# A decoder block's first stage rebuilt: x in two halves, modulation by pairs of chunks, eight accumulators, products of ones in pauses

## The chip, the cores and the metric

The kernel runs on one core of a Trainium2 chip. The metric is the device time of one execution in microseconds (us); the kernel before took 1197.91 us, the median of three runs from 1197.79 to 1198.57. The engines have one instruction queue each and run them in order: TensorE (PE in the profile; its weight loads are listed apart as PEld), VectorE (DVE), ScalarE (ACT), GpSimd (POOL) and SyncE (SP), which here issues every DMA. They wait for each other on semaphores.

## What is computed

One layer of a decoder block over 1024 tokens of width 1024. Only its opening is touched by the change:

```python
cond = jax.nn.silu(c)
mod = cond @ w_ada + b_ada                      # 6 x 1024
sh_a, sc_a, gt_a, sh_m, sc_m, gt_m = jnp.split(mod, 6)
h = rms_norm(x, g_attn_pre) * (1 + sc_a) + sh_a
proj = h @ w_in                                 # 1024 x 2304
```

Behind that stand two attention mixers over `proj`, an output projection, a residual and a squared-ReLU MLP of width 4096. All operands are float32. A product of large matrices is made of three TensorE passes, since each operand is split into a high part and the rest: high by high, high by low, low by high.

## The kernel before

The tokens lie in 8 blocks (`tb`) of 128, the model width in 8 chunks (`k`) of 128. The six units `u` of `w_in` are 384 columns wide (`UW`). A unit's projection of a block accumulates in one PSUM bank over the 8 chunks, with three products of 128x128 by 128x384 for each chunk (L771, L772 and L774 in `proj_mm`; "a triple" below). A block's accumulator is then read out by `evac` (rotary embedding, splits into high and low parts, and transposes of queries and keys on TensorE, L724 and L736), and attention starts from these with its score products (L997).

The first stage does four things. It loads x, squares it for the norm (`x_block`, L553), scales it by the norm (L558), transposes it on TensorE (eight products per block, L568) and copies it to `xnT` (L573). It loads the 2048 columns of `w_ada` that make `sh_a` and `sc_a`, and multiplies them with `cond`: partly on TensorE, as products whose moving operand has a single column (L615), partly on VectorE into `acc_a` (L626, L628), whose 128 rows are then added up by products with a column of ones (L635). Out of that come scale and shift of one chunk (L640, L641). It modulates x with them (L645) and splits the result into `hw`, high part on ScalarE (L651), low part on GpSimd (L654). And it multiplies unit 0.

Before the change, five blocks (`FIRST`) take part while `w_ada` arrives: chunk by chunk, `mod_chunk` makes the coefficients, and the five accumulators of `first_unit` take that chunk in. The remaining three blocks are transposed later, wait in PSUM for all eight chunks' coefficients (L580, L583, L593, L596) and are multiplied as ordinary tiles (`proj_tile`).

The order of instructions on each engine is not written out: `Sched` is a planner that runs when the program is built. Each step has a listed duration, dependences, buffers that it takes and gives back, and a priority; at each point the planner takes the step that can start first by its own clocks. The order that comes out is then fixed in the program. The listed durations decide only the order; on the chip each instruction waits on semaphores. TensorE's steps stand in named streams, of which `prefer` takes one first. Loads go through SyncE, in the order of the priorities from `pri()`; a load whose buffer is still in use holds up those behind it. Buffers are `stg` (3 tiles), `wa`, and `w_st` for `w_in`.

Of the kernel before, what the change touches and what calls it, by code (L numbers as in the profile page):

```python
# [134 lines left out]
class Sched:  # L135


    def __init__(self):
        self.clk = dict(PE=0.0, ACT=0.0, DVE=0.0, POOL=0.0, SP=0.0)
        self.queue = {e: [] for e in ("ACT", "DVE", "POOL", "SP")}  # L140
        self.pe = {}
        self.launch = []
        self.seq = 0
        self.dma = 0.0

# [84 lines left out]
    def run(self, prefer):  # L230
        while True:
# [72 lines left out]
def hybrid_block(ctx: ExitStack, tc: tile.TileContext, x, positions, w_ada, b_ada, g_attn_post, w_in, w_out,  # L304
# [110 lines left out]
    FIRST = 5  # L415
# [4 lines left out]
    xnT = p0.tile([P, KC, FIRST * P], F32, name="xnT")  # L420
    r_wa, r_xs, r_acc = Res(4), Res(2), Res(3)
# [6 lines left out]
    e_c = load(lambda: nc.sync.dma_start(head[:], consts[:, 0:HEAD]), 106496, prio=pri())  # L428
    wa_t, wa_e, sent = {}, {}, {}

    def load_ada(k):
        def emit():
            wa_t[k] = p0.tile([P, KC, 2, P], F32, name="wa", tag="wa", bufs=4)
            for i in range(2):
                nc.sync.dma_start(wa_t[k][:, :, i], ada_view[:, :, i * D + k * P:i * D + (k + 1) * P])

        def issued():
            sent[k].t = 0.0
        sent[k] = Ev()
        wa_e[k] = load(emit, 1048576, takes=[(r_wa, 1)], prio=pri(), after=issued)  # L440
# [3 lines left out]
    def load_x(tb, deps=()):  # L444
        r = r_stg if tb % 2 == 0 else r_xs

        def emit():
            x_t[tb] = stage("x_sb") if tb % 2 == 0 else p0.tile([P, D], F32, name="x_sb", tag="x_sb", bufs=2)
            nc.sync.dma_start(x_t[tb][:], x[tb * P:(tb + 1) * P])
        x_e[tb] = load(emit, 524288, deps, takes=[(r, 1)], prio=pri())  # L450
# [3 lines left out]
    def load_w(u, k, prio=None, deps=()):  # L454
# [13 lines left out]
        w_rawe[u, k] = load(emit, 196608, deps, takes=[(r_wst, 1)], prio=pri() if prio is None else prio)  # L468

    def split_w(u, k):  # L470
# [10 lines left out]
        if u == 0:  # L481
            w_e[u, k] = op("POOL", t_ptt(UW), lo(G), [e], gives=[(r_wst, 1)], prio=3)
# [3 lines left out]
    for tb in range(2):  # L486
        load_x(tb)
    e_posi = load(lambda: nc.sync.dma_start(posi[:], positions), 4096, prio=pri())
    load_ada(0)
    for tb in range(2, FIRST):  # L490
        load_x(tb)
    load_w(0, 0)
    for k in range(1, KC):
        load_ada(k)
        load_w(0, k)
    for tb in range(FIRST, TB):
        load_x(tb, [sent[KC - 2 if tb == FIRST else KC - 1]])

    e_init = op("DVE", 0.3, lambda: (V.memset(ones[:], 1.0), V.memset(nhalf[:], -0.5)), prio=0)
# [40 lines left out]
    def f_sin():  # L540
# [3 lines left out]
    e = op("ACT", 3.0, f_sin, [e], prio=8)  # L544
    e_rope = op("DVE", 0.15, lambda: V.tensor_scalar(sinw[:, :, 0], sinw[:, :, 1], -1.0, None, ALU.mult), [e],
                prio=8)

    e_xn = []

    def x_block(tb):  # L550
# [8 lines left out]
        box, eh, d_all, evs_ = {}, [], [], []  # L559

        def hv():
            return x_t[tb][:].rearrange("p (k t) -> p k t", k=KC)
        r_x_ = r_stg if tb % 2 == 0 else r_xs
        for g in range(2):
# [4 lines left out]
            d = pe_op("xt", 0.7, tr, [e], takes=[(r_t, 1)], gives=[(r_x_, 1)] if g and tb < FIRST else [])  # L569
            d_all.append(d)  # L570
            if tb < FIRST:
                def ev(fn, g=g):
                    return lambda: fn(xnT[:, 4 * g:4 * g + 4, tb * P:(tb + 1) * P], box[g][:])  # L573
                e_xn.append(op("ACT", t_ps(512), ev(A.copy), [d], gives=[(r_t, 1)], prio=2))
            else:
                def ev(eng, g=g):
                    def f():
                        for k in range(4 * g, 4 * g + 4):
                            if eng is A:
                                A.activation(hv()[:, k], box[g][:, k - 4 * g], AF.Identity,  # L580
                                             bias=s_a[:, k:k + 1], scale=g_a[:, k:k + 1])
                            else:
                                V.tensor_scalar(hv()[:, k], box[g][:, k - 4 * g], g_a[:, k:k + 1],  # L583
                                                s_a[:, k:k + 1], ALU.mult, ALU.add)
                    return f
                evs_.append((d, ev))
        for d, ev in evs_:

            eh.append(op(("ACT", "DVE"), (1.4, 1.3), (ev(A), ev(V)), d_all + [e_gs[k] for k in range(KC)],
                         gives=[(r_t, 1)], prio=1))  # L590
        if tb >= FIRST:
            def hi(fn):
                return lambda: fn(hw[:, tb, 0], x_t[tb][:])  # L593

            def lo(eng):
                return lambda: eng.tensor_tensor(hw[:, tb, 1], x_t[tb][:], hw[:, tb, 0].bitcast(F32), ALU.subtract)  # L596
            e = op(("ACT", "DVE"), (t_sb(D), t_d2(D)), (hi(A.copy), hi(V.tensor_copy)), eh, prio=1)
            e2 = op(("DVE", "POOL"), (t_dv(D), t_ptt(D)), (lo(V), lo(G)), [e], gives=[(r_x_, 1)], prio=1)
            e_h[tb] = [e, e2]

    e_gs, e_h, e_hh, e_hl = {}, {}, {}, {}
    NF0 = FIRST * P
    ADA_PE = (8, 2, 2, 2, 2, 2, 2, 2)

    def mod_chunk(k):
        b = {}
        e = None
        jp = ADA_PE[k]
        ej = None

        def pm0():
            b["ps"] = px.tile([P, 2], F32, name="pm", tag="x")
            for i in range(2):
                for j in range(jp):
                    T.matmul(b["ps"][:, i:i + 1], wa_t[k][:, j, i], cond[:, j:j + 1], start=(j == 0), stop=(j == jp - 1))  # L615
        if jp:
            e = pe_op("mod", 0.426 * jp, pm0, [wa_e[k], e_cond], takes=[(r_x, 1)],
                      gives=[(r_wa, 1)] if jp == KC else [])
            if jp < KC:
                ej = op("DVE", 0.07, lambda: V.tensor_tensor(bb[:, k], bb[:, k], b["ps"][:], ALU.add), [e, e_cols],  # L620
                        gives=[(r_x, 1)], prio=1)
        for j in range(jp, KC):
            def f(j=j):
                if j == jp:
                    b["acc"] = p0.tile([P, 2, P], F32, name="acc_a", tag="acc_a", bufs=3)
                    V.tensor_scalar(b["acc"][:], wa_t[k][:, j], cond[:, j:j + 1], None, ALU.mult)  # L626
                else:
                    V.scalar_tensor_tensor(b["acc"][:], wa_t[k][:, j], cond[:, j:j + 1], b["acc"][:], ALU.mult, ALU.add)  # L628
            e = op("DVE", 0.4 if j > jp else 0.26, f, [wa_e[k], e_cond] if j == jp else [e] + ([ej] if ej and j == KC - 1 else []),
                   takes=[(r_acc, 1)] if j == jp else [], gives=[(r_wa, 1)] if j == KC - 1 else [], prio=3)  # L630

        def pm():
            b["ps"] = px.tile([P, 2], F32, name="pm", tag="x")
            for i in range(2):
                T.matmul(b["ps"][:, i:i + 1], b["acc"][:, i], ones[:, 0:1], start=True, stop=True)  # L635
        if jp < KC:
            e = pe_op("misc", 0.43, pm, [e, e_init], takes=[(r_x, 1)], gives=[(r_acc, 1)])

        def gs():
            V.tensor_scalar(g_a[:, k:k + 1], b["ps"][:, 1:2], bb[:, k, 1:2], cols[:, 8 + k:9 + k], ALU.add, ALU.mult)  # L640
            V.tensor_scalar(s_a[:, k:k + 1], b["ps"][:, 0:1], bb[:, k, 0:1], None, ALU.add)  # L641
        e = e_gs[k] = op("DVE", 0.26, gs, [e, e_cols] + ([ej] if ej else []), gives=[(r_x, 1)], prio=0)
        h = xnT[:, k]
        e = op("ACT", t_sb(NF0) + 2 * AP_COST,
               lambda: A.activation(h, h, AF.Identity, bias=s_a[:, k:k + 1], scale=g_a[:, k:k + 1]),  # L645
               [e] + e_xn, prio=0)

        hb, ks = h.rearrange("p (b t) -> p b t", t=P), slice(k * P, (k + 1) * P)

        def hi(fn):  # L650
            return lambda: fn(hw[:, 0:FIRST, 0, ks], hb)  # L651

        def lo(eng):
            return lambda: eng.tensor_tensor(hw[:, 0:FIRST, 1, ks], hb, hw[:, 0:FIRST, 0, ks].bitcast(F32),  # L654
# [5 lines left out]
    for tb in range(FIRST):  # L660
        x_block(tb)
# [1288 lines left out]
```

## Time and profile before

| what | value |
|---|---|
| median of three runs | 1197.91 us |
| the profiled execution | 1197.14 us, of which its span from first to last instruction 1195.4 us |
| granted TensorE clock, mean over the span | 0.988 |
| the first product of unit 0 (acc, L771) | starts at 28.70 us |
| the first score product of attention (s_ps, L997) | starts at 86.8 us |
| the MLP's products (mlp_ps) | from 565.1 us on |

The page gives busy time by engine, a strip of 40 slices of the span, the chain of work that ended last, and groups of instructions. Times in a timeline are from the start of the span: start, duration, engine, line, operation, tile written and tiles read, count, and in brackets how long the engine had stood idle and what ended that. A float32 product with a single moving column (L615, L635) is recorded twice, so 32 records are 16 instructions. A matmul's recorded duration contains its way through the array; what a product costs in a row of them is the distance from one start to the next.

### The profile page before, as it was taken

To read this page: it belongs to the slowest core of one execution; us is meant where nothing else is said; L and a number is where in the kernel's file an instruction comes from. 1 tells how busy PE (TensorE), PEld (TensorE's weight loads), DVE (VectorE), ACT (ScalarE), POOL (GpSimd) and SP (SyncE) were. 2 spreads that over 40 slices of the span, in tenths; PEclk is the share of its full clock that TensorE was granted. 3 is DMA by queue.
4 is the path that set the end of the run, shared out by engine and by line. 5 is a ranking of instruction groups with operands and counts; after the bars stand their busy time and mean duration, and the time that the engine had idled before them with its cause. 6 is when DMAs were issued, how large, how long until landed. Compare 5 with 4: busy or idle time off the path is not lost.

```text
span 1195.4 us, 17424 instructions
## 1 busy us (share of the span) xinstructions
PE 1143.5 (96%) x6064; PEld 998.0 (83%) x6064; DVE 881.3 (74%) x1794; ACT 666.6 (56%) x1411; POOL 264.6 (22%) x325
## 2 busy tenths in 40 slices
PE   7879999999998998999899999999999999999996
PEld 6869999989998896888688888888888888888885
DVE  4977667666789897667888955479763797646998
ACT  6457666556666787667657533473325643246542
POOL 6534655465655333111100000000000000000002
PEclk9889999999999999999999999999999999999999
DMA  9621333213231422555296126952268511586103
GB/s 290 189 60 60 89 98 97 77 52 102 76 87 54 125 53 77 179 201 204 113 381 246 36 73 238 340 168 62 81 218 284 191 36 53 179 287 220 36 19 141
DMA packets 104423, 166.53 MB, mean 139 GB/s; under 512 B 11152, under 2 KB 56336, under 8 KB 104336
## 3 DMA queue, kind: packets, MB, share of 16 engines
q1 hardware_dynamic: 104336, 165.42, 41.8%
q8 instruction: 48, 0.79, 0.3%
q14 instruction: 39, 0.32, 0.1%
HBM read 137.08 MB, written 28.31 MB: 138 GB/s over the span
## 4 chain that ended last, share of the span: by engine, by line
PE 76%; DVE 13%; issue 4%; ACT 3%; POOL 3%; DMA 1%; SPq 0%; DVEq 0%; POOLq 0%; ACTq 0%
PE mlp_ps L1773 16%; PE mlp_ps L1774 16%; PE mlp_ps L1772 16%; PE pj L771 4%; PE pj L774 3%; PE pj L772 3%; PE s_ps L997 3%; PE o_ps L1131 1%; PE pt_ps L1100 1%; DVE acc_a L628 1%; PE y_ps L1348 1%; PE y_ps L1350 1%; PE pm L615 1%; PE y_ps L1349 1%; PE pt_ps L1103 1%
## 5 line engine op out<-in xcount | busy, mean ns | idle before, releaser
L1772 PE MATMUL mlp_ps<-hw 128*128 128x512 f32 x896 | 350.4, 391 | 0.4 <-ACT hw L1534 0.4
L1773 PE MATMUL mlp_ps<-hw 128*128 128x512 f32 x896 | 349.2, 390 | 1.1 <-DVE hw L1540 1.1
L1774 PE MATMUL mlp_ps<-hw 128*128 128x512 f32 x896 | 349.1, 390 | 0.0
L1773 PEld LDWEIGHTS mlp_ps<-hw 128*128 128x128 f32 x896 | 168.6, 188 | 36.9 <-DVE hw L1540 1.4
L1772 PEld LDWEIGHTS mlp_ps<-hw 128*128 128x128 f32 x896 | 168.6, 188 | 36.1 <-ACT hw L1534 0.8
L1774 PEld LDWEIGHTS mlp_ps<-hw 128*128 128x128 f32 x896 | 168.5, 188 | 35.1
L1543 DVE TENSOR_TENSOR hw<-w,hw 128x1024 fp32r<-128x1024 f32 x96 | 114.6, 1219 | 93.5 <-ACT hw L1536 93.3
L1536 ACT CAST hw<-w 128x1024 fp32r<-128x1024 f32 x96 | 97.4, 1046 | 129.9 <-PE mlp_ps L1774 93.2
L1872 POOL TENSOR_TENSOR st<-st,nhalf 128x1 f32<-128x1 f32 x8 | 7.8, 978 | 602.8 <-DVE st L1870 602.8
L771 PE MATMUL pj<-w_hl,hw 128*128 128x384 f32 x344 | 128.2, 373 | 10.0 <-DVE sk L717 10.0
L774 PE MATMUL pj<-w_hl,hw 128*128 128x384 f32 x344 | 117.4, 341 | 0.0
L772 PE MATMUL pj<-w_hl,hw 128*128 128x384 f32 x344 | 117.1, 341 | 0.0
L1536 ACT CAST hw<-u 128x1024 fp32r<-128x1024 f32 x48 | 48.6, 1051 | 64.6 <-PE mlp_ps L1774 64.6
L1118 DVE TENSOR_TENSOR ph<-pt_ps,ph 128x512 fp32r<-128x512 f32 (+1 forms) x110 | 68.8, 643 | 18.5 <-ACT ph L1114 17.6
L771 PEld LDWEIGHTS pj<-w_hl,hw 128*128 128x128 f32 x344 | 65.8, 191 | 11.8 <-issue 8.7
L1543 DVE TENSOR_TENSOR hw<-u,hw 128x1024 fp32r<-128x1024 f32 x48 | 57.0, 1217 | 18.2 <-ACT hw L1536 18.2
L1114 ACT CAST ph<-pt_ps 128x512 fp32r<-128x512 f32 (+1 forms) x110 | 59.2, 560 | 13.8 <-PE pt_ps L1103 9.8
L772 PEld LDWEIGHTS pj<-w_hl,hw 128*128 128x128 f32 x344 | 66.2, 192 | 0.8 <-issue 0.2
L774 PEld LDWEIGHTS pj<-w_hl,hw 128*128 128x128 f32 x344 | 65.7, 191 | 0.0
L1027 POOL TENSOR_SCALAR p_sb<-p_sb,den 128x128 f32<-128x128 f32 (+3 forms) x64 | 50.1, 786 | 70.2 <-DVE den L1025 46.8
L1830 DVE TENSOR_TENSOR yacc<-yacc,mlp_ps 128x512 f32<-128x512 f32 x96 | 62.1, 680 | 3.3 <-PE mlp_ps L1774 3.3
L1022 ACT ACTIVATE p_sb<-p_sb,mn 128x128 f32<-128x128 f32 (+3 forms) x64 | 49.9, 780 | 20.4 <-DVE mn L1015 16.6
(209 smaller groups left out, 2202.6 us busy)
## 6 DMA issues: line engine op xcount, KB each, us to landing
hw<-s_dram SPq DMA_DIRECT2D x84, 512.0 KB, 4.5
wa_st<-in_w_ada SPq DMA_DIRECT2D x32, 512.0 KB, 4.0
w<-in_w_up SPq DMA_DIRECT2D x32, 512.0 KB, 5.4
w<-in_w_down SPq DMA_DIRECT2D x32, 512.0 KB, 8.0
s_dram<-hw SPq DMA_DIRECT2D x28, 512.0 KB, 4.3
x_sb<-in_x SPq DMA_DIRECT2D x16, 512.0 KB, 6.2
wa<-in_w_ada SPq DMA_DIRECT2D x16, 512.0 KB, 7.0
w_st<-in_w_in SPq DMA_DIRECT2D x32, 192.0 KB, 4.7
```

Source lines behind the costliest of these rows:

```text
L771: T.matmul(ps, hw[:, tb, 0, t], w[:, 0], start=(k == 0), stop=False)
L772: T.matmul(ps, hw[:, tb, 0, t], w[:, 1], start=False, stop=False)
L774: T.matmul(ps, hw[:, tb, 1, t], w[:, 0], start=False, stop=(k == KC - 1))
L1027: lambda b=b, qi=qi: G.tensor_scalar(rec.p[qi], rec.p[qi], b["den"][:], 1.0, ALU.mult, ALU.mult), [e], prio=1))
L1114: A.copy(b["ph"][:, 0, :w], b["pt"][:, :w])
L1118: V.tensor_tensor(b["ph"][:, 1, :w], b["pt"][:, :w], b["ph"][:, 0, :w].bitcast(F32), ALU.subtract)
L1536: A.copy(out[j][0], flat(src[j]))
L1543: V.tensor_tensor(out[j][1], flat(src[j]), out[j][0].bitcast(F32), ALU.subtract)
L1772: T.matmul(ps[m][:], sh, mh, start=starts and k == 0, stop=False, **kw)
L1773: T.matmul(ps[m][:], sh, ml_, start=False, stop=False, **kw)
L1774: T.matmul(ps[m][:], sl, mh, start=False, stop=k == 3, **kw)
L1830: e = op("DVE", t_dv(512), lambda: V.tensor_tensor(y(), y(), ps[m][:], ALU.add), [e, ml.e_y[tb, n]], gives=gives, prio=1)
```

## The change

x is loaded, normed and transposed for all eight blocks: blocks 0 to 3 ahead of the first `w_ada` tiles, 4 to 7 behind the first four of them. `w_ada` arrives in 16 tiles, four for each pair of chunks, each with a quarter of the rows for that pair's 512 columns (two DMAs, in runs of 256 columns instead of 128), and the modulation is made by pairs of chunks (`mod_group`). For the first pair all of it is done by single-column products on TensorE (32), for the other three pairs half (16) and the rest on VectorE, added up by four products with ones. The transposes' copies and the modulated x are divided between ScalarE and VectorE; GpSimd has neither the low parts of `hw` nor those of unit 0's weights any more. Every load of the first stage waits for the one before it to be issued (`in_turn`) and takes `stg` or one of six `wa` places. Eight accumulators stand side by side; block 7's starts when the modulation gives back its bank; the last two chunks are taken in block by block. The sine tables come after the transposes. And before each TensorE step of this stage, a `filler` puts products of a 128x128 tile of ones wherever the planner's clock shows a pause, four at a time, written into unused columns of block 4's bank. Unit 1's weights are loaded right behind the first stage.

```diff
+            if e == "PE":
+                if self.filler:
+                    self.filler(s, name)
                 self.pe[name].pop(0)
...
-    FIRST = 5
+    FIRST = 8
+    AHEAD = 6
...
+    NWA = 6
+    order0 = [("x", t) for t in range(4)] + [(0, j) for j in range(4)] + [("x", t) for t in range(4, TB)]
+    order0 += [(g, j) for g in range(1, 4) for j in range(4)]
+    beside = {a for n, a in enumerate(order0) if n % 3 == 0}
...
+    def in_turn(emit, nbytes, ring):
+        before, mine = gone[0], Ev()
+        gone[0] = mine
+        def issued():
+            mine.t = 0.0
+        return load(emit, nbytes, [before], takes=[(ring, 1)], prio=pri(), after=issued)
...
+    BY_PE = ((0, 1, 2, 3), (2, 3), (2, 3), (2, 3))
...
+        for x in parts:
+            def mv(x=x):
+                if x == parts[0]:
+                    b["ps"] = px.tile([P, 512], F32, name="pm", tag="x")
+                for k, i in cols4:
+                    for n in range(2 if x >= 0 else 1):
+                        o = GW * i + k * P
+                        w = wa_t[g, x][:, 512 * n + o:512 * n + o + P] if x >= 0 else b["acc"][:, o:o + P]
+                        v = cond[:, 2 * x + n:2 * x + n + 1] if x >= 0 else ones[:, 0:1]
+                        T.matmul(b["ps"][:, 2 * k + i:2 * k + i + 1], w, v, ...)
+            ep = pe_op("mod", 0.9 if x >= 0 else 0.45, mv, [wa_e[g, x], e_cond] if x >= 0 else [e, e_init], ...)
...
+        eh = op("ACT", t_sb(n) + 2 * AP_COST, lambda: A.activation(hh, h, AF.Identity, bias=s_a[:, k:k + 1],
+                                                                  scale=g_a[:, k:k + 1]), deps, prio=0)
+        e = op(("DVE", "ACT"), (t_d2(n) + 2 * AP_DV, t_sb(n) + 2 * AP_COST), (full(V), full(A)), [eh], prio=0)
+        e = op("DVE", t_dv(n), lambda: V.tensor_tensor(hw[:, t0:t1, 1, ks], h, hh.bitcast(F32), ALU.subtract), [e],
+               prio=0)
...
+    def filler(start, name):
+        t = max(sc.clk["PE"], (e_init.t or start) + 0.2)
+        n = max(0, int((start - t - 0.06) / 0.24))
+        if e_init.t is not None and st.d == 0:
+            n = max(n, 1)
+        for _ in range(4 * n):
+            T.matmul(accs[FILL][:, UW:], ones_r[:], ones_r[:], start=not fill.open, stop=not fill.open)
...
+        order = [(k, part, tb) for x in (0, 1) for k in range(2) for part in range(2)
+                 for tb in (range(4) if x == 0 else range(4, 7))]
+        order += [(k, part, tb) for k in range(2, AHEAD) for part in range(2) for tb in range(7)]
+        order += [(k, part, 7) for k in range(AHEAD) for part in range(2)]
+        order += [(k, part, tb) for tb in (7, 0, 1, 2, 3, 4, 5, 6) for k in range(AHEAD, KC) for part in range(2)]
```

In the program that comes out of it, TensorE's queue stands in this order. "Products" are those with a single moving column, fillers are products of ones, transposes are counted singly, and part products are those of unit 0 (three to a triple): 100 fillers; block 0's 8 transposes with 32 fillers among and behind them; block 1's 8 with 8 fillers; pair 0's 32 products, with the 16 transposes of blocks 2 and 3 and 28 fillers between them; 24 fillers; 8 part products with 12 fillers, then 16 fillers; 16 part products with 24 transposes; 16 fillers; pair 1's 20 products with block 7's 8 transposes; 24 fillers; 39 part products with pair 2's 20 products and 16 fillers; 6 part products; pair 3's 20 products; 123 part products, among them the first two blocks' transposes of `evac`. That is 92 products (58 before) and 276 fillers.

More of the change, by code (lines that the diff above doesn't have):

```diff
@@ L481, in split_w, with f_init @@
         if u == 0:
-            w_e[u, k] = op("POOL", t_ptt(UW), lo(G), [e], gives=[(r_wst, 1)], prio=3)
+            w_e[u, k] = op("DVE", t_dv(UW), lo(V), [e], gives=[(r_wst, 1)], prio=3)
         else:
             w_e[u, k] = op(("DVE", "POOL"), (t_dv(UW), t_ptt(UW)), (lo(V), lo(G)), [e], gives=[(r_wst, 1)], prio=3)
-    for tb in range(2):
+    load_x(0)
+    e_posi = load(lambda: nc.sync.dma_start(posi[:], positions), 4096, prio=pri())
+    for tb in range(1, 4):
         load_x(tb)
[L488 to L499, printed above, removed]
+    for g in range(4):
+        for j in range(4):
+            load_ada(g, j)
+        for k in range(2):
+            load_w(0, 2 * g + k)
+        if g == 0:
+            for tb in range(4, TB):
+                load_x(tb)
+    ones_r = p0.tile([P, P], F32R, name="ones_r")
+    fill = Tok()
+    fill.open = False
+    def f_init():
+        V.memset(ones[:], 1.0)
+        V.tensor_copy(ones_r[:], ones[:])
+        V.memset(nhalf[:], -0.5)
+    e_init = op("DVE", 0.4, f_init, prio=0)
     e = op("ACT", 0.1, lambda: A.activation(cond[:], c_raw, AF.Exp, scale=-1.0), [e_c], prio=0)
@@ L587, in x_block @@
[L587 to L605, printed above, removed]
-        b = {}
[L607 to L637, printed above, removed]
-        def gs():
[L640 to L654, printed above, removed]
-                                             ALU.subtract)
-        e_hh[k] = op("ACT", t_sb(NF0), hi(A.copy), [e], prio=0)
-        e_hl[k] = op("POOL", t_ptt(NF0), lo(G), [e_hh[k]], prio=0)
-        split_w(0, k)
@@ L660, in hybrid_block, with ev @@
-    for tb in range(FIRST):
-        x_block(tb)
-    for k in range(KC):
-        mod_chunk(k)
-    for tb in range(FIRST, TB):
-        x_block(tb)
+            d = pe_op("xt", 0.43, tr, [e], takes=[(r_t, 1)], gives=[(r_x_, 1)] if g else [])
+            def ev(fn, g=g):
+                return lambda: fn(xnT[:, 4 * g:4 * g + 4, tb * P:(tb + 1) * P], box[g][:])
+            e_xn[tb // 4].append(op(("ACT", "DVE"), (t_ps(512), t_dv(512)), (ev(A.copy), ev(V.tensor_copy)), [d],
+                                    gives=[(r_t, 1)], prio=2))
@@ L777, in tick @@
         st.d += 1 / (TB * KC)
[L779 to L794 removed]
+    FILL, accs = 4, {}
@@ new lines, in filler, with emit, after @@
+    def filler(start, name):
[5 more added lines that the diff above has]
+            T.matmul(accs[FILL][:, UW:], ones_r[:], ones_r[:], start=not fill.open, stop=not fill.open)
+    sc.filler = filler
+    def first_unit():
+        order = [(k, part, tb) for x in (0, 1) for k in range(2) for part in range(2)
[3 more added lines that the diff above has]
+        order += [(k, part, tb) for tb in (7, 0, 1, 2, 3, 4, 5, 6) for k in range(AHEAD, KC) for part in range(2)]
+        last = {k: x for x, (k, _, _) in enumerate(order)}
+        accs[FILL] = acc_at[FILL][0].tile([P, 512], F32, name="acc", tag=acc_at[FILL][1])
+        acc_at[FILL][2].free.pop()
+        for x, (k, part, tb) in enumerate(order):
+            pl, tag, r = acc_at[tb]
+            first = k == 0 and part == 0 and tb != FILL
+            def emit(k=k, part=part, tb=tb, pl=pl, tag=tag, first=first):
+                if first:
+                    accs[tb] = pl.tile([P, 512], F32, name="acc", tag=tag)
+                fill.open |= tb == FILL
+                proj_mm(accs[tb][:, :UW], k, w_hl[0, k], tb, part)
+            def after(k=k, part=part, tb=tb):
+                if part:
+                    tick()
+                if k == KC - 1:
+                    sc.filler = None
+            d = dense(0.346 if part == 0 else 0.173, emit,
+                      [w_e[0, k], (e_hl if part else e_hh)[k, tb // 4]] + (e_xn[0] + e_xn[1] if tb > 4 else []),
+                      takes=[(r, 1)] if first else [], after=after, gives=[(r_w, 1)] if last[k] == x else [])
+            if k == KC - 1 and part:
+                yield (0, tb, lambda tb=tb: accs[tb], d, r)
```

154 lines of the change are left out of this document (91 added, 63 removed).

## The prediction

> **What bounds the kernel now.** I read the page first, for the engine that the end hangs on.
>
> ```profile
> span 1195.4 us, 17424 instructions
> ...
> PE 1143.5 (96%) x6064; PEld 998.0 (83%) x6064; DVE 881.3 (74%) x1794; ACT 666.6 (56%) x1411; POOL 264.6 (22%) x325
> ...
> PE 76%; DVE 13%; issue 4%; ACT 3%; POOL 3%; DMA 1%; SPq 0%; DVEq 0%; POOLq 0%; ACTq 0%
> ```
>
> TensorE is busy for 96% and holds 76% of the chain. So a stage is worth the TensorE time that stands idle in it. Windows cut at the stage's events show where that is (columns: stretch, its length, busy time and records of PE, PEld, DVE, ACT, POOL, then clock, DMA share, GB/s).
>
> ```profile
> 10.00:38.00 28.00, 25.46 (x122) 24.10 (x121) 17.94 (x40) 17.77 (x31) 17.31 (x32) 1.00 1.15 307
> 38.00:62.00 24.00, 21.13 (x121) 20.20 (x120) 21.20 (x39) 10.88 (x18) 14.04 (x11) 0.86 0.44 136
> 62.00:77.20 15.20, 8.37 (x53) 7.49 (x51) 14.37 (x47) 8.09 (x28) 6.85 (x4) 0.88 0.38 108
> ...
> 110.00:350.00 240.00, 236.02 (x1694) 228.99 (x1693) 170.42 (x591) 149.77 (x450) 134.66 (x148) 0.99 0.29 84
> 350.00:470.00 120.00, 108.91 (x712) 100.09 (x711) 109.03 (x360) 90.90 (x296) 49.59 (x72) 1.00 0.28 78
> ```
>
> From 110 to 350 us TensorE is full (236 of 240); from 350 to 470 VectorE nearly is (109 of 120). Ahead of 77 us the loads end near 48, then VectorE leads (21.2 of 24, 14.4 of 15.2) and TensorE idles for 10 us. That idle time is what a better first stage could win. So the question is what TensorE's own queue costs once all eight blocks run in it. Its timeline has the prices.
>
> ```profile
> 10.24 6.83 PE L615 MATMUL pm<-cond,wa 128*128 128x1 f32 x32
> 16.93 4.68 PE L568 MATMUL pxt<-head,x_sb 128*128 128x128 f32 x20
> ...
> 30.77 0.52 PE L771 MATMUL acc<-w_hl,hw 128*128 128x384 f32 x1
> 31.09 0.52 PE L772 MATMUL acc<-w_hl,hw 128*128 128x384 f32 x1
> ...
> 34.72 0.33 PE L772 MATMUL acc<-w_hl,hw 128*128 128x384 f32 x1
> 34.89 0.33 PE L771 MATMUL acc<-w_hl,hw 128*128 128x384 f32 x1
> ...
> 37.21 0.61 PE L635 MATMUL pm<-ones,acc_a 128*128 128x1 f32 x4 [1.46 <-DVE acc_a L628]
> ...
> 39.46 1.63 PE L774 MATMUL acc<-w_hl,hw 128*128 128x384 f32 x4
> ...
> 52.10 0.95 PE L615 MATMUL pm<-cond,wa 128*128 128x1 f32 x8
> 52.91 0.42 PE L771 MATMUL acc<-w_hl,hw 128*128 128x384 f32 x1
> ...
> 57.71 1.07 PE L568 MATMUL pxt<-head,x_sb 128*128 128x128 f32 x8
> 58.53 0.42 PE L771 MATMUL acc<-w_hl,hw 128*128 128x384 f32 x1
> ```
>
> The engine has two rates. Part products start 0.32 us apart at 31 us and 0.17 apart at 34.7. A single-column product costs 6.83/16 = 0.43 us at the low rate (32 records are 16 instructions), and (52.91-52.10)/4 = 0.20 at the high one. A transpose costs 4.68/20 = 0.235 and (58.53-57.71)/8 = 0.10, of which I take 0.12 to allow for its waits. Neither holds the high rate: 16 products and 20 transposes ran without a pause from 10.24 to 21.6 at the low one, and only part products raised it.
>
> **The change, part by part.** The step's own listed price for eight single-column products is 0.9 us, half of what the rows give (1.6, or 3.4 at the low rate). The planner ordered by that price, and the queue is in order. It has 92 such products in place of 58, so I add up that queue.
>
> Fillers (128x128, new): no row has them. The nearest are the transposes of queries and keys, of the same size and type:
>
> ```profile
> 78.28 0.41 PE L724 MATMUL pq<-ident_r,sp 128*128 128x128 f32 x2
> 78.49 0.65 PE L771 MATMUL pj<-w_hl,hw 128*128 128x384 f32 x1
> ...
> 83.14 0.46 PE L736 MATMUL pk<-ident_r,sk 128*128 128x128 f32 x4
> 83.44 0.41 PE L771 MATMUL pj<-w_hl,hw 128*128 128x384 f32 x1
> ```
>
> That gives 0.21/2 = 0.105 and 0.30/4 = 0.075. Packed, I take 0.067 at the high rate (0.17 for 384 columns bounds it from below at 0.058); both ends stay in the range.
>
> The rate is the unknown. For stretches with few part products I take the middle between both rates, for others the high one.
>
> - To block 1's last transpose: start 1.3, the first 100 fillers 8.5 (6.7 to 10.5), 16 transposes 1.9, 40 fillers 2.7. Sum 14.4 us. x is there by then.
> - Pair 0: 32 products, 16 transposes, 28 fillers: 6.4+1.9+1.9 = 10.2 at the high rate, 13.8+3.8+2.9 = 20.5 at the low one. Middle 15.4: to 29.8.
> - 52 fillers and 8 part products: 3.5+1.4 to 5.5+2.6. Take 6.3 (mostly low): to 36.1. Beside it lie pair 0's coefficients and the modulation of the first half.
> - 16 part products, 24 transposes, waits 0.4, 16 fillers: 2.8+2.9+0.4+1.1 = 7.2: to 43.3. Blocks 4 to 7 are scaled by VectorE only behind the first half's modulation. Each x tile's place goes to a `w_ada` tile, so SyncE's queue now stands behind these transposes. I price that at nothing: the last tile's place is freed near 50 by pair 1's products, and its own products stand at 66 in the sum. With a landing of 4 to 7 us (below) that is covered; beyond some 9 us of delay it costs directly.
> - Pair 1: 20 products and 8 transposes: 5.0 or 10.5. Middle 7.7: to 51.0.
> - 24 fillers 2.4 (pair 1's coefficients and two casts hide them): to 53.4.
> - 39 part products 6.7, 20 products 4.0, 16 fillers 1.1: 11.8, to 65.2.
> - 6 part products and pair 3's 20 products: 5.0, to 70.2.
> - 123 part products 21.3, two pairs of `evac` transposes 0.9, waits for their readout 2.8 (0 to 5): to 95.2.
>
> The loads and the engines that could hold this up:
>
> ```profile
> wa_st<-in_w_ada SPq DMA_DIRECT2D x32, 512.0 KB, 4.0
> ...
> wa<-in_w_ada SPq DMA_DIRECT2D x16, 512.0 KB, 7.0
> ```
>
> ```profile
> L1543 DVE TENSOR_TENSOR hw<-w,hw 128x1024 fp32r<-128x1024 f32 x96 | 114.6, 1219 | 93.5 <-ACT hw L1536 93.3
> ```
>
> ```profile
> 57.03 1.00 DVE L628 SCALAR_TENSOR_TENSOR acc_a<-wa,cond,acc_a 128x256 f32<-128x256 f32 x2
> ...
> 63.95 0.74 DVE L558 TENSOR_SCALAR x_sb<-x_sb,rstd 128x1024 f32<-128x1024 f32 x1
> ```
>
> VectorE takes over the low parts (1.22 each). From pair 1's coefficients at 51.5 to the last chunk's low part it has: sums of half tiles, 0.5 for 256 columns and so 0.8 for 512 (8 of them, 6.4); six low parts (7.3) and two halves (1.2); four full modulations at 0.74 (3.0) and two halves (0.8); six weight splits, 1.22 x 384/1024 = 0.46 each (2.8); coefficients 1.5. That is 23.0, so about 74.5 us, while TensorE comes to that part product past 83 (80 part products behind 70.2). Hidden, with 9 us of cover. GpSimd's old low parts go; nothing waited there at the end.
>
> Before, at the same work: block 6's last part product stood at 90.28, with 7 blocks done.
>
> ```profile
> 77.18 0.66 PE L771 MATMUL pj<-w_hl,hw 128*128 128x384 f32 x1 [5.56 <-DVE sk L717]
> ...
> 90.28 0.33 PE L774 MATMUL pj<-w_hl,hw 128*128 128x384 f32 x1
> ...
> 90.72 1.17 PE L997 MATMUL s_ps<-kt,qt 128*128 128x256 f32 x8
> ```
>
> By 90.6 it had done 56 triples, 8 score products (1.2) and some 0.5 more of `evac` transposes. The eighth block is 8 x 0.52 = 4.2, so the same work stands at 90.6+4.2-1.7 = 93.1. The new stage ends 95.2-93.1 = 2.1 us later.
>
> Then attention starts later against the products: now 28 part products of unit 1 (4.8 us) stand between unit 0's last and the first score product; before, the first came 6 us ahead of that mark. That lag of 11 us is free while TensorE is full, but fewer part products are left for the stretch from 350 to 470, where VectorE leads. I take the 4.8 of them (0 to 11). Sum: +6.9.
>
> The span becomes 1202.3. The profiled execution lies 1.74 over its span (1197.14) and the median 0.77 over that: **1205 us**.
>
> **The clock rule, weighed.** The product at 39.46 runs at the low rate (1.63 for four), though the longest pause ahead of it was 1.46 us. The Trainium skill ("TensorE: Matmul & The Clock Gate", "Part 1: The HAM clock gate") has the rate rise after a busy window of about 3.4 us and fall after an idle one. By that alone the 100 fillers would set the high rate for the whole stage, rival 2's time; this trace shows it fall without such a pause.
>
> **The rivals.**
>
> 1. *The products cost what the step lists*, 0.11 each (say, since two of the same column follow each other). Then pair 0 takes 7.3 (8.1 less), pair 1 3.2 (4.5 less), the other 40 products 3.6 less: 16.2 less, **1189 us**, faster. It decides where a product costs under 0.15. Against it stand both rows, 16 and 4 of them in a row. The Trainium skill ("TensorE: Matmul & The Clock Gate", "LDWEIGHTS (loading the stationary operand)") has columns / 1.2 ns for a weight load, an estimated 107 ns here, which would speak for it; the row measures 0.20 at best.
> 2. *The fillers hold the high rate throughout.* Pair 0 5.2 less, pair 1 2.7 less: **1197 us**, no change; without the lag 1192. For it: 100 in a row are as dense as part products. Against: between the transposes they come four at a time, 0.3 us in some 2.
> 3. *The low rate holds up to the dense part products at 70 us.* Pair 0 5.2 and pair 1 2.8 more, 40 products at 0.23 and 45 part products at 0.15 more (16): **1229 us** as its end, and 1220 where the 45 part products raise the rate again halfway.
>
> **How the numbers follow.** Forecast 0.62 (own range 1199 to 1212), rival 1 0.10, rival 2 0.14, rival 3 0.14. The range, 1193 to 1221, leaves out most of rival 1 and the upper half of 3. A difference under 0.2% (2.4 us) can't be told from none. Slower by more: 0.94 of the forecast and rival 3, 0.73. Faster: rival 1 and a third of rival 2, 0.14. Within: 0.13.
>
> **What would show it.** Eight products with `cond` in a row over 1.5 us; the first part product of unit 0 near 32 us, not ahead of 28.7; loads pausing between 17 and 40; the last part product of unit 0 near 95, the first score product near 100. It is wrong if the products cost half, if DMA and VectorE hold up the tail instead, or if attention ends no later than its start shifts.

## The result, and the profile after

The changed kernel takes 1251.95 us (median of four runs, 1244.86 to 1252.99); the kernel before took 1198.24 beside it (1197.79 to 1199.15). The ratio is 1.0435, with a 95% interval of 1.0396 to 1.0474. The forecast was 1205, the end of the range 1221: slower was right, the size was not.

The page after (span, TensorE's busy time, and the costliest of the new groups):

```profile
span 1250.4 us, 18091 instructions
...
PE 1216.8 (97%) x6408; PEld 1071.4 (86%) x6408; DVE 865.6 (69%) x1761; ACT 665.6 (53%) x1402; POOL 238.4 (19%) x309
...
L815 PE MATMUL acc<-ones_r 128*128 128x128 f32 x276 | 60.6, 404 | 1.3 <-DVE ones_r L537 1.3
```

TensorE works 73.3 us more than before, and the products with ones are 60.6. TensorE's timeline of the changed kernel shows what one costs:

```profile
1.30 21.60 PE L815 MATMUL acc<-ones_r 128*128 128x128 f32 x100 [1.30 <-DVE ones_r L537]
...
22.69 1.08 PE L601 MATMUL pxt<-head,x_sb 128*128 128x128 f32 x4
...
34.29 3.51 PE L648 MATMUL pm<-cond,wa 128*128 128x1 f32 x16
37.67 1.09 PE L815 MATMUL acc<-ones_r 128*128 128x128 f32 x4
...
62.11 0.63 PE L798 MATMUL acc<-w_hl,hw 128*128 128x384 f32 x1
...
78.27 1.98 PE L815 MATMUL acc<-ones_r 128*128 128x128 f32 x16
80.08 1.89 PE L648 MATMUL pm<-cond,wa 128*128 128x1 f32 x16
...
139.70 0.35 PE L801 MATMUL acc<-w_hl,hw 128*128 128x384 f32 x1
```

From 1.30 to 22.69, 100 of them take 21.4 us, 0.214 each; the first transpose waits behind them. Only in one short stretch at the high rate are they 0.113 ((80.08-78.27)/16). Windows cut at the steps of the prediction's sum (busy time of PE, PEld, DVE, ACT, POOL, then clock, DMA share, GB/s):

```profile
0.00:22.69 22.69, 21.39 (x100) 21.39 (x101) 2.52 (x15) 7.02 (x11) 4.24 (x16) 1.00 0.72 231
...
85.89:91.05 5.16, 5.16 (x26) 5.16 (x25) 5.12 (x10) 4.75 (x6) 0.00 (x0) 0.50 1.10 337
...
sum 139.90, PE 137.84 PEld 136.51 DVE 47.02 ACT 46.42 POOL 28.42; mean PE 15.32 PEld 15.17 DVE 5.22 ACT 5.16 POOL 3.16
```

TensorE is busy for 137.84 of the stage's 139.90 us while VectorE works 47: the stage is nothing but TensorE's queue. The clock column reads 0.50 where 24 products with ones take 0.215 each, but 1.00 in the first row, where they take the same 0.214. So in this trace it says nothing about the rate until its first change; the distances of the starts do.

| step of the sum | predicted us | measured us | ones in it, predicted | ones in it, measured |
|---|---|---|---|---|
| to pair 0's first product | 14.4 | 34.3 | 11.2 | 30.1 |
| pair 0 | 15.4 | 22.7 | 2.4 | 6.2 |
| 52 ones, 8 part products | 6.3 | 13.7 | 4.4 | 10.7 |
| 16 part products, 24 transposes, 16 ones | 7.2 | 9.4 | 1.1 | 1.8 |
| pair 1 | 7.7 | 5.8 | 0 | 0 |
| 24 ones | 2.4 | 5.2 | 2.4 | 5.2 |
| to pair 3's last product | 16.8 | 22.8 | 1.1 | 2.6 |
| 123 part products and `evac` | 25.0 | 26.0 | 0 | 0 |
| sum: end of unit 0 | 95.2 | 139.9 | 22.6 | 56.6 |

The measured column is the distance between starts in the timeline, and of the ones in a step their runs are added up in the same way; the ones predicted are the middles of the terms given there, or the share that the step took of its range (4.4 of 3.5 to 5.5). The stage ends 44.7 us later than forecast: 34.0 for the ones, and 10.7 net for the rest, most of it other work at the low rate where the middle or the high one was taken. Behind the stage lie 1250.4-139.9 = 1110.5 us, against 1107.1 forecast: 3.4 more. 44.7+3.4 is the whole miss (1250.4 against 1202.3). The first score product comes at 145.4 us (86.8 before), the MLP's products begin at 619.8 (565.1): the loss is made in the first stage and kept.

### The profile page after: what moved, and what is told of

Its sections match the earlier page's. It is cut to its first block, busy times and chain, and to the rows that moved or that the text cites. A ratio compares the mean times of both kernels' runs of the same rounds, so it can differ in the third digit from the quotient of the medians.

```text
span 1250.4 us, 18091 instructions
## 1 busy us (share of the span) xinstructions
PE 1216.8 (97%) x6408; PEld 1071.4 (86%) x6408; DVE 865.6 (69%) x1761; ACT 665.6 (53%) x1402; POOL 238.4 (19%) x309
## 4 chain that ended last, share of the span: by engine, by line
PE 79%; DVE 11%; issue 3%; ACT 3%; POOL 3%; DMA 1%; SPq 0%; DVEq 0%; POOLq 0%; ACTq 0%
PE mlp_ps L1829 15%; PE mlp_ps L1830 15%; PE mlp_ps L1828 15%; PE acc L815 4%; PE pj L798 3%; PE pj L799 3%; PE pj L801 3%; PE s_ps L1053 2%; PE pm L648 2%; PE o_ps L1187 1%; DVE ph L1174 1%; PE acc L798 1%; PE pt_ps L1156 1%; PE acc L799 1%; PE y_ps L1404 1%
## 5 line engine op out<-in xcount | busy, mean ns | idle before, releaser
L798 PE MATMUL pj<-w_hl,hw 128*128 128x384 f32 x320 | 118.7, 371 | 1.8 <-DVE sk L744 1.8
L799 PE MATMUL pj<-w_hl,hw 128*128 128x384 f32 x320 | 109.1, 341 | 0.0
L801 PE MATMUL pj<-w_hl,hw 128*128 128x384 f32 x320 | 109.1, 341 | 0.0
L798 PEld LDWEIGHTS pj<-w_hl,hw 128*128 128x128 f32 x320 | 61.3, 192 | 2.8 <-DVE sk L744 2.2
L799 PEld LDWEIGHTS pj<-w_hl,hw 128*128 128x128 f32 x320 | 61.6, 192 | 0.7 <-POOL w_hl L509 0.2
L815 PE MATMUL acc<-ones_r 128*128 128x128 f32 x276 | 60.6, 404 | 1.3 <-DVE ones_r L537 1.3
L801 PEld LDWEIGHTS pj<-w_hl,hw 128*128 128x128 f32 x320 | 61.2, 191 | 0.0
```

Of the source, the lines that this page charges most:

```text
L798: T.matmul(ps, hw[:, tb, 0, t], w[:, 0], start=(k == 0), stop=False)
L799: T.matmul(ps, hw[:, tb, 0, t], w[:, 1], start=False, stop=False)
L801: T.matmul(ps, hw[:, tb, 1, t], w[:, 0], start=False, stop=(k == KC - 1))
L815: T.matmul(accs[FILL][:, UW:], ones_r[:], ones_r[:], start=not fill.open, stop=not fill.open)
```

## The experiments

Each is timed beside the kernel before on the same chip (its medians there lie from 1197.97 to 1200.51 us, so times of different experiments are compared to some 2 us only), and all differ from the changed kernel only by what is shown or named. Each trace is of one execution.

**1. No products with ones.**

```diff
-        for _ in range(4 * n):
-            T.matmul(accs[FILL][:, UW:], ones_r[:], ones_r[:], ...)
+        return
```

> All 276 products with ones left out, everything else in the changed kernel's order. Theory F (the ones' products are the loss): they held TensorE for some 57 us (100 in 21.4 us, 24 in 5.2 us, 16 in 1.8 us), ahead of work that was ready. Without them the stage is bound by the 92 single-column products at 0.42 (39 us), 64 transposes at 0.18 (12 us) and the part products (33 to 45 us), or by the loads; the first score product comes near 95 to 105 in place of 145, time 1200 to 1212. Rival P (the chunk products and the new order are the loss, and the ones only fill time in which TensorE would have waited): the first score product stays past 130, time 1235 or more.

1204.65 us (1203.72 to 1205.48), ratio 1.0061 [1.0042, 1.0079]. TensorE's timeline of this kernel:

```profile
7.95 1.97 PE L601 MATMUL pxt<-head,x_sb 128*128 128x128 f32 x8 [7.95 <-DVE rs_t L412]
...
12.56 3.41 PE L648 MATMUL pm<-cond,wa 128*128 128x1 f32 x16
15.83 1.95 PE L601 MATMUL pxt<-head,x_sb 128*128 128x128 f32 x8
...
30.73 0.69 PE L798 MATMUL acc<-w_hl,hw 128*128 128x384 f32 x1 [1.42 <-ACT hw L678]
...
95.15 0.35 PE L801 MATMUL acc<-w_hl,hw 128*128 128x384 f32 x1
```

x is ready at 7.95, and unit 0 ends at 95.4 in place of 139.9; the first score product comes at 100.9, in place of 145.4. Its window to 95.40 has TensorE busy for 83.00, so 12.4 us idle; in the changed kernel it was 2.1. So 10.3 of the 56.6 us of ones filled real waits, and the other 46.3 held up work: about the 47.3 us between the two kernels, 44.5 of them in the stage. Theory F stands, rival P falls. What is left is 0.6% over the kernel before.

**2. The same number in bf16.**

```diff
-    ones_r = p0.tile([P, P], F32R, name="ones_r")
+    ones_r = p0.tile([P, P], BF16, name="ones_r")
```

> The same 276 products with ones, in bf16 in place of fp32r, still 128 columns. Theory F1 (a 128-column fp32r product is charged like 256 columns: 0.214 at the low rate, 0.113 at the high one): in bf16 100 of them take 10.7 us in place of 21.4, the sum halves, time near 1224 if the rate stays low, near 1205 if they now raise it (a single-column product then at 0.20 to 0.22 at 25 us). Rival F2 (0.214 is the price of issuing any product back to back at the low rate): 100 still take 21 us, time 1250.

1203.71 us (1201.05 to 1211.08), ratio 1.0048 [1.0028, 1.0069]. TensorE's timeline of this kernel:

```profile
1.30 7.59 PE L815 MATMUL acc<-ones_r 128*128 128x128 bf16 x100 [1.30 <-DVE ones_r L537]
8.72 0.61 PE L601 MATMUL pxt<-head,x_sb 128*128 128x128 f32 x4
...
9.84 1.73 PE L815 MATMUL acc<-ones_r 128*128 128x128 bf16 x28
11.40 0.60 PE L601 MATMUL pxt<-head,x_sb 128*128 128x128 f32 x4
...
12.73 1.90 PE L648 MATMUL pm<-cond,wa 128*128 128x1 f32 x16
14.49 0.38 PE L815 MATMUL acc<-ones_r 128*128 128x128 bf16 x4
...
23.90 2.72 PE L815 MATMUL acc<-ones_r 128*128 128x128 bf16 x24
26.38 0.67 PE L798 MATMUL acc<-w_hl,hw 128*128 128x384 f32 x1
```

100 take 7.4 us, not 21.4, and 28 of them 1.56, 0.056 each. Single-column products now stand at (14.49-12.73)/8 = 0.22: the rate has risen. By 23.90 it has fallen again (24 at 0.103), with fillers of four between transposes and products all along. Rival F2 (any product costs 0.214) falls.

**3. The same number, 256 moving columns.** They are columns of zeros, added over half of block 4's bank.

```diff
-            T.matmul(accs[FILL][:, UW:], ones_r[:], ones_r[:], ...)
+            w = P if fill.open and not fill.wide else 2 * P
+            fill.wide |= fill.open
+            T.matmul(accs[FILL][:, 512 - w:], ones_r[:], zero_r[:, :w], ...)
```

> The same 276 products with 256 columns (of zeros, added to the same accumulator) in place of 128 of ones. Theory F1 (128 columns are charged like 256, and leave half of the time unused, too little to raise the rate): the price at a rate stays the same, 0.214 or 0.107, but the rate rises within the first 100, which take 11 to 15 us in place of 21.4; single-column products at 0.22 in place of 0.42; time 1195 to 1215. If width does not matter for the rate: 100 still take 21.4 us, time 1250. Rival F2 (price by columns, 0.0017 a column at the low rate): 100 take 43 us, time 1290 or more.

1219.85 us (1214.73 to 1222.04), ratio 1.0182 [1.0151, 1.0212]. TensorE's timeline of this kernel:

```profile
1.90 14.47 PE L821 MATMUL acc<-zero_r,ones_r 128*128 128x256 f32 x100 [1.90 <-DVE zero_r L541]
16.21 0.60 PE L605 MATMUL pxt<-head,x_sb 128*128 128x128 f32 x4
...
22.73 1.84 PE L652 MATMUL pm<-cond,wa 128*128 128x1 f32 x16
24.43 0.72 PE L821 MATMUL acc<-zero_r,ones_r 128*128 128x256 f32 x4
...
34.88 3.12 PE L821 MATMUL acc<-zero_r,ones_r 128*128 128x256 f32 x24
37.83 0.34 PE L802 MATMUL acc<-w_hl,hw 128*128 128x384 f32 x1
...
56.25 5.46 PE L821 MATMUL acc<-zero_r,ones_r 128*128 128x256 f32 x24
61.52 0.37 PE L802 MATMUL acc<-w_hl,hw 128*128 128x384 f32 x1
```

Twice the columns, and 100 take 14.3 us, a third less than with half the columns: the rate rises within them, and products stand at (24.43-22.73)/8 = 0.21. At that rate one of 256 columns costs 2.95/24 = 0.123, where one of 128 cost 0.113. By 56.25 the rate has fallen again, and there one of 256 costs 5.27/24 = 0.22, where one of 128 cost 0.214. That fitted F1, and the rival that prices by columns (43 us for 100) falls. Its time lay above what I expected: unit 0 ends only at 110.4, and TensorE is busy for 107.7 us of that. But it doesn't tell a charge for narrow products from one that doesn't depend on the moving columns at all, which experiment 4 does.

**4. 64 stationary columns.** What put F1 in doubt is the single-column products above: 16 records in 3.38 us, 0.21 for each pass, the price of the ones with a single moving column.

```diff
-            T.matmul(accs[FILL][:, UW:], ones_r[:], ones_r[:], ...)
+            T.matmul(accs[FILL][:64, UW:], ones_r[:, :64], ones_r[:], ...)
```

> The 276 fp32r products with ones as in the changed kernel, with 64 stationary columns in place of 128 and the same 128 moving columns (64 output rows). Theory W (what is paid is the load of the stationary operand: a record with 1, with 128 and with 256 moving columns took 0.21 us alike at the low rate): half as many stationary columns cost half, 100 take 10.7 us or less in place of 21.4; time 1205 to 1226, by whether the rate rises too. Theory F1 (fewer than 256 moving columns are charged like 256): the price stays at 0.214, 100 take 21.4 us, time 1250.

1201.95 us (1197.88 to 1205.22), ratio 1.0021 [1.0007, 1.0035], below the 1205 to 1226 that I expected. TensorE's timeline of this kernel:

```profile
1.30 8.83 PE L815 MATMUL acc<-ones_r 128*64 128x128 f32 x100 [1.30 <-DVE ones_r L537]
9.97 0.62 PE L601 MATMUL pxt<-head,x_sb 128*128 128x128 f32 x4
...
11.05 1.93 PE L815 MATMUL acc<-ones_r 128*64 128x128 f32 x28
12.81 0.62 PE L601 MATMUL pxt<-head,x_sb 128*128 128x128 f32 x4
...
28.30 2.80 PE L815 MATMUL acc<-ones_r 128*64 128x128 f32 x24
30.90 0.54 PE L798 MATMUL acc<-w_hl,hw 128*128 128x384 f32 x1
```

The moving columns and the type are those of the changed kernel, and 24 cost 0.108 each at the low rate in place of 0.215, 28 at the high one 0.063 in place of 0.113. F1, my first explanation, falls; theory W holds: a pass costs the longer of its weight load and its moving columns, and an fp32r load of 128 columns is 0.214 us at the low rate, as long as 256 of a part product's moving columns (0.32 for 384). The records of the weight loads go the same way: the shortest of the ones' is 0.190 us in the changed kernel, 0.133 with 64 columns, 0.095 in bf16. (64 stationary columns also mean 64 output rows; but the bf16 ones have 128 rows at 0.103, so the rows are not what is paid for.) The rate rises here as well.

**5. The planner's price for them put right.**

```diff
-        n = max(0, int((start - t - 0.06) / 0.24))
+        n = max(0, int((start - t - 0.06) / 0.86))
```

> The fp32r products with ones stay as they are, but the planner lists four of them at 0.86 us (0.214 each, as measured) in place of 0.24 when it divides a pause by their price: 108 of them are issued in place of 276. Theory F: the time goes with their number times 0.214 where nothing else was late. Between none (1204.65) and 276 (1251.95) that gives 47.3 x 108/276 = 18.5 us over none: 1223, with 1212 as the lower end where some of them fill real waits. Rival: the first long run of them alone is the loss (100 in a row, now 28): then 1210 or less.

1219.61 us (1213.07 to 1225.69), ratio 1.0177 [1.0143, 1.0212], near the 1223 of theory F and above the 1210 of its rival. TensorE's timeline of this kernel:

```profile
1.30 6.24 PE L815 MATMUL acc<-ones_r 128*128 128x128 f32 x28 [1.30 <-DVE ones_r L537]
...
12.48 0.64 PE L815 MATMUL acc<-ones_r 128*128 128x128 f32 x4
12.96 0.62 PE L601 MATMUL pxt<-head,x_sb 128*128 128x128 f32 x4
```

The trace, of the fastest of the four executions (1213.07), is less clear than the time. Unit 0 ends at 104.1, 8.7 us later than with no ones, not 18.5; the first 28 end before x is ready, so the loss is in the later ones, but it is not 0.214 times their number. And here the same fp32r ones stand where the rate rises, with transposes and no part product among them: 28 cost some 0.22 each, the four at 12.48 cost 0.12.

**6 and 7. Fewer single-column products on TensorE, bf16 ones.** Experiment 6 as shown, 7 with `(3,)` for the first pair too.

```diff
-    BY_PE = ((0, 1, 2, 3), (2, 3), (2, 3), (2, 3))
+    BY_PE = ((2, 3), (3,), (3,), (3,))
```

> bf16 ones, and of the four tiles of w_ada per pair TensorE multiplies two, one, one, one in place of four, two, two, two; VectorE sums the others. Theory Q (with the ones cheap, the single-column products in TensorE's in-order queue are what is left): 40 products fewer, at 0.22 to 0.42 each 9 to 17 us less on TensorE, and 7 us more on VectorE, which sat idle from 15 to 24 us; first score product at 84 to 90 in place of 96, time 1194 to 1200. Rival V (VectorE and the loads bound the stage once the ones are cheap): first score product no earlier than 94, time 1203 or more.

> As the run before, with one tile of four on TensorE in every pair. Theory Q: 8 products fewer again (2 to 3 us of TensorE), but pair 0's coefficients now wait for VectorE's sum of three tiles (4.2 us behind the last landing): between no change and 2 us earlier than with two tiles. Rival V: later than with two tiles by 1 us or more.

Experiment 6: 1191.65 us (1185.92 to 1197.2), ratio 0.9934 [0.991, 0.9958]; experiment 7: 1190.97 (1188.99 to 1193.45), 0.992 [0.9894, 0.9946]. Both beat the kernel before. The groups of products, of experiment 2, then of experiment 7 (busy us, mean ns, then idle time ahead):

```profile
L648 PE MATMUL pm<-cond,wa 128*128 128x1 f32 x160 | 20.2, 256 | 0.0
```

```profile
L648 PE MATMUL pm<-cond,wa 128*128 128x1 f32 x64 | 9.3, 275 | 0.0
L648 PE MATMUL pm<-ones,acc_a 128*128 128x1 f32 x32 | 4.8, 271 | 1.1 <-DVE acc_a L631 1.1
```

Unit 0 ends at 89.9 in experiment 6 and at 84.7 in experiment 7, against 90.7 in experiment 2. The time of experiment 6 came as theory Q has it, its first score product did not: 95.5, no earlier than rival V's 94. V's reason isn't seen either: of the 89.9 us TensorE is busy for 86.8 and VectorE for 54.9, and the planner has put 320 ones into the shorter queue in place of 276. The medians of experiments 2 and 6 lie 12.1 us apart, the spans of their profiled executions 7.0, and 6.2 of these lie behind the first stage (1102.3 us from unit 0's end to the span's, 1108.5 in experiment 2).

**8. Fewer products, no ones** (the edits of experiments 1 and 6 together).

> Two, one, one, one tiles on TensorE as above, and no products with ones at all. It tells what the bf16 ones are worth where fewer products need the high rate. If the rate theory holds (products and transposes run at half the rate without dense work beside them): 52 products and 64 transposes at the low rate cost up to 52 x 0.2 + 64 x 0.12 = 18 us more, of which the waits hide a part: 2 to 8 us later than with bf16 ones. If the stage is bound by loads: the same within 2 us.

1201.33 us (1199.45 to 1203.46), ratio 1.0011 [0.9996, 1.0025]: 9.7 more than experiment 6, where I had expected 2 to 8. Yet unit 0 ended at 87.2, 2.7 earlier than there; the loss lay behind the stage. By this run alone the bf16 ones don't pay in their own stage.

**9. The measured prices in the planner's list, with one tile of four and bf16 ones; 10. the same without ones.**

```diff
-            ep = pe_op("mod", 0.9 if x >= 0 else 0.45, ...)
+            ep = pe_op("mod", 1.76 if x >= 0 else 0.88, ...)
```

> One tile of four on TensorE, bf16 ones, and the planner's list corrected: eight single-column products at 1.76 us and four at 0.88, the measured high-rate price, in place of 0.9 and 0.45. Theory Q: the queue's order follows the real times better, and the waits of 2.0, 0.5 and 1.1 us ahead of transposes and sums shrink: 1187 to 1191. Rival: the order was good enough, and longer listed products only shift the pauses: within 2 us of 1191.

> One tile of four on TensorE, the measured prices of the single-column products in the list, and no products with ones. It asks whether the best version needs them. With bf16 ones the last part product of unit 0 stood at 82.9 us and the time was 1189.08. Theory K (they pay by keeping the rate up for 48 products and 64 transposes): last part product at 86 or later, time 1193 or more. Rival (few products are left that the rate helps, and 316 ones cost as much as they save): last part product at 80 to 84, time 1186 to 1192.

Experiment 9: 1189.08 us (1188.11 to 1191.33), ratio **0.9908 [0.9885, 0.9931]**, the lowest, though its interval overlaps those of experiments 6 and 7. Experiment 10: 1195.94 (1191.34 to 1199.46), 0.998 [0.9963, 0.9997]. Groups of experiment 9 to 83 us, then of experiment 10 to 84 us:

```profile
L601 PE MATMUL pxt<-head,x_sb 128*128 128x128 f32 x64 | 9.3, 276 | 2.0 <-ACT x_sb L593 2.0
L648 PE MATMUL pm<-cond,wa 128*128 128x1 f32 x64 | 7.7, 250 | 0.0
L648 PE MATMUL pm<-ones,acc_a 128*128 128x1 f32 x32 | 4.0, 247 | 0.0
```

```profile
L601 PE MATMUL pxt<-head,x_sb 128*128 128x128 f32 x64 | 13.8, 388 | 11.4 <-DVE x_sb L594 7.6 <-ACT x_sb L593 3.1 <-ACT xnT L605 0.7
L648 PE MATMUL pm<-cond,wa 128*128 128x1 f32 x64 | 12.6, 326 | 0.0
L648 PE MATMUL pm<-ones,acc_a 128*128 128x1 f32 x32 | 5.6, 297 | 1.8 <-DVE acc_a L631 1.8
```

With ones, transposes and products take 21.0 us of TensorE, without them 32.0, and unit 0 ends at 83.1 or at 86.5. Here theory K holds: cheap ones pay 3.4 us in the stage, and the median is lower by 6.9. In experiments 6 and 8 the stage went the other way by 2.7, so what ones are worth in it hangs on the rest of the queue; how is not shown. What the price list itself gave (experiment 9 against experiment 7, 1.6 us in the stage and 1.9 in the median) is within the spread of these runs.

**11. The low parts of h given back to GpSimd**, where the planner likes, in experiment 7's kernel.

```diff
-        e = op("DVE", t_dv(n), lambda: V.tensor_tensor(hw[...], h, hh.bitcast(F32), ALU.subtract), [e], prio=0)
+        e = op(("DVE", "POOL"), (t_dv(n), t_ptt(n)), (low(V), low(G)), [e], prio=0)
```

> One tile of four on TensorE, bf16 ones, and the low parts of h may go to GpSimd where the planner has it free (before, all of them did). VectorE was busy for 8.5 and 8.8 of 10 us from 40 to 60. Theory V2 (VectorE now bounds the tail of the stage): last part product of unit 0 2 to 4 us earlier, time 1187 to 1189. Rival: the sums wait for w_ada's landing and TensorE is full (10 of 10 from 40 to 60), so the same within 2 us, or later where a GpSimd low part of 2 us stands ahead of a part product.

1194.27 us (1192.77 to 1195.18), ratio 0.9944 [0.9925, 0.9962]: 3.3 more than experiment 7, and unit 0 ends at 88.3, 3.6 later. Groups of this kernel:

```profile
L682 POOL TENSOR_TENSOR hw<-xnT,hw 128x512 fp32r<-128x512 f32 (+1 forms) x7 | 14.3, 2041 | 28.0 <-DVE xnT L676 28.0
...
L682 DVE TENSOR_TENSOR hw<-xnT,hw 128x1024 fp32r<-128x1024 f32 x3 | 5.7, 1913 | 0.0
```

Theory V2 falls: seven low parts take GpSimd 14.3 us, and of VectorE's own three, two take 1.21 and 1.22 us and the one beside a low part of GpSimd 3.31, where one of 1024 columns in experiment 7 takes 1.23:

```profile
68.13 1.23 DVE L681 TENSOR_TENSOR hw<-xnT,hw 128x1024 fp32r<-128x1024 f32 x1
```

Nothing here speaks for giving them back. Why the stage is longer is not shown: TensorE's idle time in it is the same (5.8 us against 5.7), but it is busy for 82.6 us in place of 79.1, at a granted clock of 0.86 in place of 0.92.

## Why the prediction was right about the sign and wrong about the size

**The step that failed** is the price of the fillers: "The nearest are the transposes of queries and keys ... Packed, I take 0.067 at the high rate (0.17 for 384 columns bounds it from below at 0.058); both ends stay in the range." It was mis-sized by 34.0 us: 22.6 forecast, 56.6 measured. Three things were wrong in it. 0.067 lies under what the runs show at the high rate, 0.113: a part product hides its weight load beneath 384 moving columns, and so it is no bound for one with 128. 0.105, the price for the low rate, is half of the 0.214 measured, and nearly all of the ones ran at that rate. And 100 in a row were priced at 8.5 us, between the two, though the same text said that it took part products to raise the rate.

Both prices came of stopping at the start of the next product. The rows behind it, in the trace of before, show that part of the cost falls between this product and the one after it:

```profile
78.94 0.52 PE L772 MATMUL pj<-w_hl,hw 128*128 128x384 f32 x1
79.26 0.52 PE L774 MATMUL pj<-w_hl,hw 128*128 128x384 f32 x1
...
83.69 0.33 PE L772 MATMUL pj<-w_hl,hw 128*128 128x384 f32 x1
```

From 78.49 to 78.94 are 0.45, where part products at this rate stand 0.32 apart, and from 83.44 to 83.69 are 0.25 in place of 0.17. With that remainder a transpose costs (78.94-78.28-0.32)/2 = 0.17 at the low rate and (83.69-83.14-0.17)/4 = 0.095 at the high one. Longer rows with the price stood in the prediction: 32 records of single-column products in 6.83 us are 0.213 each, with one moving column, and it priced a transpose of x, of the fillers' size, at 0.235.

**The middle rate** was the second miss, the larger part of the 10.7 us. Pair 0's own work took 16.5 without its ones, against 13.0 forecast, and the way to pair 3's last product 20.2 against 15.7; pair 1, at the high rate, took 1.9 less. The 6.3 taken for the 52 fillers, called mostly low, lies below the middle of its 4.9 to 8.1; 13.7 were measured. Rival 3 (the low rate holds) was nearer than the forecast. Rival 2 (the fillers hold the high rate) is true of other ones, and for a time: those of experiments 2 and 4 held it to 22 and 21 us, those of 3 to 55; those of the change never raised it. The Trainium skill ("TensorE: Matmul & The Clock Gate", "Part 1: The HAM clock gate") has the rate rise after a busy window of about 3.4 us. Experiment 2 agrees: with 0.103 and 0.056 as its two prices, 7.4 us for 100 puts the rise some 4 us from their start. The changed kernel doesn't: 21.4 us without a pause didn't raise it. Why is open.

**Products.** 0.43 and 0.20 forecast, 0.42 ((37.67-34.29)/8) and 0.22 measured: right, and rival 1 falls. Having 52 or 48 of them in place of 92 is the only edit between experiment 2 and experiments 6 and 7; in the first stage it is worth 0.8 and 6.0 us, and the rest of the 12.1 and 12.7 between the medians lies elsewhere.

**The loads, VectorE and GpSimd** were priced at nothing, and rightly for this kernel. SyncE's queue shows the pause that was named as a sign:

```profile
12.37 25.80 SPq L477 DMA_DIRECT2D x_sb<-in_x  x4
```

Four x tiles take 25.8 us to go out, for want of a place, but TensorE, at 2.1 us of idle time in the stage, was later still. Of the other signs, the eight products in a row came (3.4 us); the first part product came at 62.1 and not near 32, unit 0's last at 139.7 and not near 95.

**The lag of attention** was taken as 4.8 us (0 to 11) on the 1102.3 us behind the equal mark of before. The changed kernel has 8.2. The others have from 0.0 (experiment 6) to 9.0 (experiment 8), without order by the length of the first stage. So up to 9 us of any of these times come from how attention falls into step, which no run here explains; a difference in time under that is not by itself read as the first stage's. The forecast's "slower" hung for 4.8 of its 6.9 us on this term, and 2.1 on the stage; measured, the stage's 46.8 (139.9 against 93.1) decide it.

**Experiment 1's 1204.65** is the forecast's 1205 by coincidence: it has none of the 22.6 us of ones in the forecast's sum, and instead 12.4 us of waits and the low rate.

## What to carry to other kernels

Price a matmul by the longer of two things, the load of its stationary operand and its moving columns, and look for that price in long rows whose moving columns are few; a row with many moving columns hides the load, and a row of two or four leaves part of its cost to the product behind it. A filler in an in-order queue costs its full price wherever the planner saw a pause that the chip doesn't have, so make it of the cheapest kind that still raises the rate, and measure whether it does. And when an operation has no row, give its range an end at each rate.

## What the hardware showed that I had not expected

- A pass with 128 stationary columns of float32 or fp32r takes 0.21 us at the low rate with 1 and with 128 moving columns and 0.22 with 256, and at the high rate 0.11 with 1 (0.22 for the two passes of a product), 0.113 with 128, 0.123 with 256. With 64 stationary columns and 128 moving ones it is 0.108 and 0.063, in bf16 with 128 of both 0.103 and 0.056.
- 100 fp32r products of 128 by 128 by 128 without a pause, 21.4 us, left the rate low; with 256 moving columns, 64 stationary ones, or bf16 it rose within the first 100. In the first case the moving columns need half of the time of the load, in the others they fill it. That this share is what counts fits these four kernels, but not experiment 5, where the ones of the first case, with transposes among them, stood where the rate rose at some 12 us. What raises the rate stays open.
- The granted clock in these traces reads 1.00 until its first change, whatever the rate: 0.214 and 0.113 for a product with ones both stand beside it.
